# Drains in the loop, paired gathers and a reordered tail in a hard-max attention kernel

## The chip, the cores and the metric

The kernel runs on one core of a Trainium2 chip. The metric is device time in microseconds, the median of several executions. Each kernel was also run once under the hardware profiler. Runs are compared only with runs of the kernel before on the same chip, in the same rounds. Some of the experiments fell on chips that ran everything at a mean granted TensorE clock of 0.90 to 0.94 in place of about 0.95, where the kernel before takes 504 to 513 us; I call them slow chips. A drain (DRAIN in the traces) is an instruction of GpSimd's sequencer that ends only some time after the gathers issued before it.

## The reference

For each of 4 batches there are 4096 queries and 4096 keys of 128 numbers. Each query takes the value row of the key with the largest dot product.

```python
logits = np.matmul(q, k.transpose(0, 2, 1))
best = np.argmax(logits, axis=-1)
return v[b_idx, best, :].astype(np.float32)
```

## The kernel before

The queries are worked off in 128 tiles of 128 rows, one tile `t` per loop iteration `it`. TensorE and ScalarE make a score for each group of four keys, VectorE folds two halves (`fold`, tile `W`) and takes the top eight (`top`, MAX8 into `TOP`). Then three kinds of indirect DMA follow, all issued by GpSimd:

- `kg`: the group's key differences, two tiles to a group, one DMA for each tile. VectorE multiplies them with the queries (`dots`, tile `prod`) and picks the key.
- `vr`: the chosen value rows, one DMA per tile ("values").
- at the very end, rows flagged as too close are done over exactly: `FR` (their records), `FQ` (their queries), `FK` (three DMAs, candidate keys), `FV` (the exact value) and a scatter into the output. Between `FV` and the scatter stands a branch to a general path that runs only if something could not be handled (with this data it never runs).

A Python scheduler fixes the order on each engine at build time. Queues `near_q` (group gathers and their completion marks), `late_q` (values) and `fast` (flagged rows) are emptied by `issue`, once per iteration:

```python
def issue(it):
    n = 0
    clock[0] = it
    put_out(it)
    while near_q and (n < 1 + (it >= T - 28 and len(near_q) > 2) or near_q[0] in marks):
        g = near_q.pop(0)
        n += g not in marks
        g()
    if fast and it >= rest[0]:
        fast.pop(0)()
        rest[0] = it + 3
    take_late(2 if n == 0 and len(late_q) > 4 or it >= T - 24 and it % 2 == 0 else 1)
```

The condition is looked at anew for each gather: when one pair with its mark is queued (three entries), the first is issued, two entries are left, and the second has to wait for the next iteration. The mark that follows the second gather lets the group's products go into VectorE's order a fixed number of iterations later:

```python
def dots(c, x, m):
    ...
    yield "until", lambda: ("kg", x) in done, 1 if x >= TAIL else 2
    kg = kg_t.pop(x)
    prod = rp.tile([P, m, 3, P], FP16, tag=f"prod{m}", name=f"prod_{x}")
    nc.vector.tensor_tensor(out=prod, in0=kg, in1=natq[b % 2][...], op=OP.mult)
    ...
```

The end, cut:

```python
        late(LATE)                       # LATE = 8 values
        get(FR, rec, rr, P * T)
        get(FQ, q_flat, row, P * T)
        late(1)
        ...
        for r in range(3):
            get(FK[:, r, :], k_flat, gb[:, r:r + 1], B * Sk)
        ...
        late(3)
        win = whole(exact(FK, FQ, gb, 3, "fe"))
        get(FV, v_flat, win, B * Sk)
        late(1 << 20)
        ...
        all_rows()                       # reads HARD, branches
        nc.gpsimd.indirect_dma_start(out=out_flat, out_offset=IOA(ap=rowk, axis=0), in_=FV, ...)
```

## Time and profile before

| | before |
|---|---|
| time, median of the first runs | 466.72 us (466.47 to 467.32) |
| span of the profiled run | 465.5 us |
| last MAX8 starts (end of the loop) | 420.1 us |
| gather FR starts | 435.2 us |
| scatter starts | 454.4 us |
| GpSimd's last long DRAIN ends | 464.7 us |

The end of the loop, in VectorE's timeline (start and duration, in us):

```profile
420.06 1.23 DVE L232 MAX8 TOP<-W 128x8 f32<-128x1024 f32 x1
```

The page of the kernel before: busy time and share of the span of each engine, then the busy tenths in 40 slices of 11.6 us.

```profile
span 465.5 us, 6396 instructions
...
PE 380.2 (82%) x1834; PEld 168.3 (36%) x1834; DVE 417.8 (90%) x825; ACT 376.8 (81%) x437; POOL 318.1 (68%) x345
...
DVE  2689999999999999999999999999998999998330
...
POOL 8233557877677888776678876677777777767730
```

VectorE (DVE) is full from the third slice to the end of the loop. GpSimd (POOL) shows 7 or 8 tenths, and looks free. It is not: each gather costs it another 0.3 us that is not counted as busy. The timeline of GpSimd, in columns start, duration, engine, line, operation, tiles and, in brackets, the idle time before it and what ended it:

```profile
303.90 0.99 POOL L304 DMA_INDIRECT vr<-in_v_dram,win  x1 [0.30 <-issue]
305.68 0.95 POOL L250 DMA_INDIRECT kg<-k,cand  x1 [0.79 <-issue]
306.94 0.99 POOL L304 DMA_INDIRECT vr<-in_v_dram,win  x1 [0.30 <-issue]
```

One gather every 1.3 us. The same view for the tail:

```profile
441.73 1.00 POOL L498 DMA_INDIRECT FK<-in_k_dram,gb_e  x1 [0.30 <-issue]
443.03 1.04 POOL L304 DMA_INDIRECT vr<-in_v_dram,win  x1 [0.30 <-issue]
444.37 1.00 POOL L304 DMA_INDIRECT vr<-in_v_dram,win  x1 [0.30 <-issue]
447.55 1.00 POOL L498 DMA_INDIRECT FV<-in_v_dram,xw_fe  x1 [2.19 <-DVE hi L573]
454.42 1.03 POOL L534 DMA_INDIRECT out_dram<-FV,rowk_e  x1 [5.87 <-issue]
```

The last gather of values ends at 445.4, FV starts when VectorE has the index (tile `xw_fe`, ready at 447.29; the view names an instruction just behind it), and the scatter starts 5.87 us after FV's end. The span ends 10 us after the scatter was issued, though no engine is busy. What lies in these holes are instructions of GpSimd's sequencer. The view of one source line lists them, with minimum, median and maximum in ns and the first and last start. First the line of the branch, then the end of the program:

```profile
L576 POOLq INC_SWDGE_SEM  x1: 2410/2410/2410, 450.8 to 450.8; - x1
```

```profile
L806 POOLq DRAIN  x3: 46/109/10489, 454.2 to 465.2; - x3
```

A semaphore instruction takes 2.41 us, from 450.8. Of the three drains at the end, the longest takes 10.49 us: it starts at 454.19, runs while the scatter is issued (until 455.45) and ends at 464.68, 9.23 us after. I measure drains in this way throughout: from the end of the last gather or load that GpSimd issued before them to their own end.

VectorE's waits for group gathers, in columns engine, line, what for, us in total, times, longest:

```profile
DVE prod L265 <- DMA kg<-k,cand: 3.9, 3, 1.8
```

### The profile page before, as it was taken

Reading aid. Unit: us, or ns where it says so; the run is one execution under the profiler, and the core shown is the slowest. Engines: PE = TensorE matmul, PEld = TensorE weight load, DVE = VectorE, ACT = ScalarE, POOL = GpSimd, SP = SyncE. Lnnn points to the kernel's source line nnn. Section 1 sums busy time; section 2 is a strip of 40 time slices with the busy share of each in tenths; the row PEclk is TensorE's granted clock in tenths of the full one; section 3 lists DMA queues with packets and bytes.
Section 4 is the critical chain, followed back from the end, with each engine's and each line's share of the span. In section 5 each row is a group of like instructions: output and inputs, shape, how many; then the busy total and the mean of one; then the engine's idle time right before and its main releaser. Section 6 shows DMA issues by size and latency. Waiting matters only on the chain.

```text
span 465.5 us, 6396 instructions
## 1 busy us (share of the span) xinstructions
PE 380.2 (82%) x1834; PEld 168.3 (36%) x1834; DVE 417.8 (90%) x825; ACT 376.8 (81%) x437; POOL 318.1 (68%) x345
## 2 busy tenths in 40 slices
PE   8999999998999889999998889998998888850100
PEld 4444444443444344444443334443333333320000
DVE  2689999999999999999999999999998999998330
ACT  2999999999999989999997889999998888840000
POOL 8233557877677888776678876677777777767730
PEclk9999999999999999999999999999999999995555
DMA  7934576853325877943235653423432333322320
GB/s 130 227 66 96 107 103 97 139 120 85 80 76 135 148 140 128 121 126 81 79 98 137 129 116 94 100 80 87 110 101 79 86 86 99 87 71 68 94 74 4
DMA packets 43624, 47.54 MB, mean 102 GB/s; under 512 B 25000, under 2 KB 33451, under 8 KB 43584
## 3 DMA queue, kind: packets, MB, share of 16 engines
q0 software_dynamic: 18752, 30.97, 33.7%
q1 hardware_dynamic: 24832, 16.13, 13.1%
q8 instruction: 14, 0.23, 0.2%
q14 instruction: 26, 0.21, 0.2%
HBM read 39.59 MB, written 12.19 MB: 111 GB/s over the span
## 4 chain that ended last, share of the span: by engine, by line
DVE 31%; issue 23%; ACT 13%; PE 13%; DMA 9%; POOL 7%; POOLq 0%; DVEq 0%; ACTq 0%
DVE W L228 14%; ACT A L202 10%; PE psn L193 5%; DVE TOP L232 5%; PE psn L212 4%; DMA kg<-k,cand 4%; ACT E L215 4%; DMA vr<-in_v_dram,win 3%; DVE prod L265 3%; PE pd L193 3%; POOL kg L250 3%; POOL vr L304 2%; DVE D L274 2%; DVE p L269 2%; DMA natk<-in_k_dram 2%
## 5 line engine op out<-in xcount | busy, mean ns | idle before, releaser
L202 ACT ACTIVATE A<-pd 128x1024 f16<-128x1024 f32 x256 | 258.6, 1041 | 23.0 <-PE pd L193 22.7
L250 POOL DMA_INDIRECT kg<-k,cand x128 | 127.4, 995 | 85.1 <-issue 26.6
L228 DVE SCALAR_TENSOR_TENSOR W<-psn,E 128x1024 int16<-128x1024 f32 x128 | 166.0, 1297 | 7.0 <-ACT E L215 5.5
L193 PE MATMUL pd<-kT,qT 128*128 128x512 f16 x512 | 151.8, 378 | 15.7 <-ACT A L202 14.8
L193 PE MATMUL psn<-kT,qT 128*128 128x512 f16 x512 | 151.8, 378 | 15.3 <-ACT A L202 7.9
L304 POOL DMA_INDIRECT vr<-in_v_dram,win x128 | 136.6, 1067 | 39.0 <-issue 37.5
L193 PEld LDWEIGHTS <-qT 128*128 128x128 f16 x1024 | 98.4, 97 | 163.9 <-issue 76.0
L232 DVE MAX8 TOP<-W 128x8 f32<-128x1024 f32 x128 | 155.8, 1217 | 0.0
L212 PE MATMUL psn<-A,identh 128*128 128x512 f16 x512 | 152.1, 378 | 0.0
L215 ACT ACTIVATE E<-psn 128x1024 int16<-128x1024 f32 x128 | 132.2, 1033 | 5.0 <-PE psn L212 5.0
L212 PEld LDWEIGHTS <-identh 128*128 128x128 f16 x512 | 49.6, 97 | 60.8
L265 DVE TENSOR_TENSOR prod<-kg,natq 128x768 f16<-128x768 f16 x64 | 34.9, 546 | 3.9 <-DMA kg<-k,cand 3.9
L269 DVE TENSOR_TENSOR p<-prod 128x384 f16<-128x384 f16 x64 | 22.3, 349 | 0.1
L274 DVE TENSOR_REDUCE D<-p 128x6 f32<-128x192 f16 x64 | 21.5, 336 | 0.1
L173 ACT ACTIVATE kT<-uk 128x256 f16<-128x256 f32 x48 | 20.1, 419 | 0.9 <-PE uk L170 0.9
L64 POOL DMA_DIRECT2D natk<-in_k_dram x27 | 16.1, 599 | 0.9 <-POOLq L795 0.8
L67 POOL DMA_DIRECT2D natq<-in_q_dram x27 | 16.3, 605 | 0.2
L169 PE MATMUL uk<-identh,natk 128*128 128x128 f16 x96 | 15.8, 218 | 0.6 <-ACT A L202 0.6
L272 DVE TENSOR_TENSOR p<-p 128x192 f16<-128x192 f16 x64 | 15.7, 245 | 0.0
L464 PE MATMUL fp_e<-n_e,tri 128*128 128x1 f32 x2 | 0.6, 361 | 16.7 <-DVE n_e L462 16.7
L170 PEld LDWEIGHTS <-natk 128*128 128x128 f16 x96 | 9.3, 97 | 7.7 <-issue 5.3
L169 PEld LDWEIGHTS <-natk 128*128 128x128 f16 x96 | 9.3, 97 | 5.6
(147 smaller groups left out, 133.5 us busy)
## 6 DMA issues: line engine op xcount, KB each, us to landing
out_dram<-vr SPq DMA_DIRECT2D x32, 256.0 KB, 2.2
natq<-in_q_dram POOLq DMA_DIRECT2D x26, 128.0 KB, 3.2
k<-kd SPq DMA_DIRECT2D x8, 384.0 KB, 4.2
natk<-in_k_dram POOLq DMA_DIRECT2D x24, 128.0 KB, 3.9
kg<-k,cand POOLq DMA_INDIRECT x128, 2.8
vr<-in_v_dram,win POOLq DMA_INDIRECT x128, 2.8
natq<-in_q_dram POOLq DMA_DIRECT2D x1, 768.0 KB
natk<-in_k_dram POOLq DMA_DIRECT2D x1, 512.0 KB, 5.2
```

What stands on the lines that cost most here:

```text
L169: nc.tensor.matmul(out=o, lhsT=natk[b % 2][:, h, 4 * m + x, :], rhs=identh, start=True, stop=False)
L193: nc.tensor.matmul(out=ps[:, n * 512:(n + 1) * 512], lhsT=qT[b % 2][:, qt * P:(qt + 1) * P], rhs=kT[b % 2][:, u * 1024 + n * 512:u * 1024 ...
L202: nc.scalar.activation(out=A, in_=ps, func=AF.Abs)
L212: nc.tensor.matmul(out=ps[:, n * 512:(n + 1) * 512], lhsT=identh, rhs=A[:, n * 512:(n + 1) * 512], start=False, stop=True)
L215: nc.scalar.activation(out=E, in_=ps, func=AF.Relu, scale=QSCALE)
L228: nc.vector.scalar_tensor_tensor(out=W_t[t % NW].bitcast(I16)[:, 1::2], in0=ps, scalar=QSCALE, in1=E, op0=OP.mult, op1=OP.max)
L232: nc.vector.max(out=TOP[:, t, :], in_=W_t[t % NW].bitcast(FP32))
L250: near_q.append(lambda j=j: nc.gpsimd.indirect_dma_start(out=kg[:, j].rearrange("p f d -> p (f d)"), out_offset=None, in_=k16[t0 // NQT], ...
L265: nc.vector.tensor_tensor(out=prod, in0=kg, in1=natq[b % 2][:, x - b * NQT:x - b * NQT + m, :].unsqueeze(2).to_broadcast([P, m, 3, P]), op ...
L269: nc.vector.tensor_tensor(out=p1, in0=prod[:, :, :, 0:64], in1=prod[:, :, :, 64:128], op=OP.add)
L274: nc.vector.tensor_reduce(out=d[:, x - c0:x - c0 + m, 1:4], in_=p2, axis=AX_X, op=OP.add)
L304: late_q.append(lambda j=j: nc.gpsimd.indirect_dma_start(out=vr[:, j, :], out_offset=None, in_=v_flat, in_offset=IOA(ap=win[:, i + j:i + j ...
```

## The change

The intent: drains in the loop, each covering an iteration in which GpSimd is given nothing else, so that the drain at the end has less to do; group gathers in pairs when the queue is behind; the branch ahead of FV, so that its cost overlaps VectorE's exact products; the last two tiles gathered singly, so that one need not wait for the other's MAX8; the flags' first steps before the last products.

```diff
+DRAINS = (28, 60, 92)
-LATE = 8
+LATE = 7
...
-        late(3)
-        win = whole(exact(FK, FQ, gb, 3, "fe"))
-        get(FV, v_flat, win, B * Sk)
         late(1 << 20)
+        hi = fp.tile([1, 1], mybir.dt.int32, tag="hi")
+        nc.vector.tensor_copy(out=hi, in_=HARD[0:1, :])
...
-        all_rows()
+        win = whole(exact(FK, FQ, gb, 3, "fe"))
+        all_rows(hi)
+        get(FV, v_flat, win, B * Sk)
         nc.gpsimd.indirect_dma_start(out=out_flat, out_offset=IOA(ap=rowk, axis=0), in_=FV, in_offset=None,
...
@@ def issue(it)
-        while near_q and (n < 1 + (it >= T - 28 and len(near_q) > 2) or near_q[0] in marks):
+        if it in DRAINS:
+            nc.gpsimd.drain()
+            owed[0] += 2
+            return
+        behind = len(near_q) > (2 if it >= T - 28 else 4)
+        while near_q and (n < 1 + behind or near_q[0] in marks):
...
-        take_late(2 if n == 0 and len(late_q) > 4 or it >= T - 24 and it % 2 == 0 else 1)
+        more = n == 0 and len(late_q) > 4 or it >= T - 24 and it % 2 == 0
+        if owed[0] and n < 2 and it % 3 == 0 and len(late_q) > 2:
+            owed[0] -= 1
+            more = True
+        take_late(2 if more else 1)
...
@@ def gathers(t)
-            if t0 <= t < t1 and ((t - t0) % 2 or t == t1 - 1):
-                x = t0 + (t - t0) // 2 * 2
-                gather(c, x, t - x + 1)
+            m = 2 if t < T - 2 else 1
+            if t0 <= t < t1 and (t - t0) % m == m - 1:
+                gather(c, t - m + 1, m)
...
     top(T - 2)
+    gathers(T - 2)
+    flush()
     fold(T - 1)
     top(T - 1)
-    gathers(T - 2)
     gathers(T - 1)
...
         while dot:
-            two, dot = dot[:2], dot[2:]
+            if last and len(dot) == 2:
+                flags_first(T // 2, T)
+            two, dot = (dot[:1], dot[1:]) if last else (dot[:2], dot[2:])
```

Cut: tile shapes that let single and paired tiles share buffers, and bookkeeping of what is done.

More of the change, by code (lines that the diff above doesn't have):

```diff
@@ L245, in gather @@
                                 op0=OP.bitwise_and, op1=OP.bitwise_xor)
-        kg = rp.tile([P, n, 3, P], FP16, tag=f"kg{n}", name=f"kg_{t0}", bufs=8)
+        kg = rp.tile([P, 2, 3, P], FP16, tag="kg", name=f"kg_{t0}", bufs=8)[:, 0:n]
         assert len(kg_t) < 8
@@ L263, in dots @@
         kg = kg_t.pop(x)
-        prod = rp.tile([P, m, 3, P], FP16, tag=f"prod{m}", name=f"prod_{x}")
+        prod = rp.tile([P, 2, 3, P], FP16, tag="prod", name=f"prod_{x}")[:, 0:m]
         nc.vector.tensor_tensor(out=prod, in0=kg, in1=natq[b % 2][:, x - b * NQT:x - b * NQT + m, :].unsqueeze(2).to_broadcast([P, m, 3, P]),
@@ L267, in dots @@
         yield "dve",
-        p1 = rp.tile([P, m, 3, 64], FP16, tag=f"p1{m}", name=f"p1_{x}")
+        p1 = rp.tile([P, 2, 3, 64], FP16, tag="p1", name=f"p1_{x}")[:, 0:m]
         nc.vector.tensor_tensor(out=p1, in0=prod[:, :, :, 0:64], in1=prod[:, :, :, 64:128], op=OP.add)
         yield "dve",
-        p2 = rp.tile([P, m, 3, 32], FP16, tag=f"p2{m}", name=f"p2_{x}")
+        p2 = rp.tile([P, 2, 3, 32], FP16, tag="p2", name=f"p2_{x}")[:, 0:m]
         nc.vector.tensor_tensor(out=p2, in0=p1[:, :, :, 0:32], in1=p1[:, :, :, 32:64], op=OP.add)
@@ L274, in dots @@
         nc.vector.tensor_reduce(out=d[:, x - c0:x - c0 + m, 1:4], in_=p2, axis=AX_X, op=OP.add)
-        done.add(("dot", x))
+        done.update(("dot", i) for i in range(x, x + m))
     def pick(c, t0, t1):
@@ L280, in pick @@
         d = D_t[c % 4][:, 0:n, :]
-        yield "until", lambda: all(("dot", x) in done for x in range(t0, t1, 2)), 0
+        yield "until", lambda: all(("dot", x) in done for x in range(t0, t1)), 0
         cand = cand_t.pop(c)
@@ L557, in exact @@
         yield "dve", 0.17
-        win = fp.tile([P, 1], U32, tag="xw", name=f"xw_{name}")
+        win = fp.tile([P, 1], U32, tag=f"xw{R}", name=f"xw_{name}")
         nc.vector.tensor_reduce(out=win, in_=lt, axis=AX_X, op=OP.min)
@@ L569, in whole, with all_rows @@
                 return s.value
-    def all_rows():
-        hi = fp.tile([1, 1], mybir.dt.int32, tag="hi")
-        nc.vector.tensor_copy(out=hi, in_=HARD[0:1, :])
+    def all_rows(hi):
         left = nc.values_load(hi[0:1, 0:1], min_val=0, max_val=1 << 24,
@@ L679, in issue @@
             rest[0] = it + 3
-        take_late(2 if n == 0 and len(late_q) > 4 or it >= T - 24 and it % 2 == 0 else 1)
+        more = n == 0 and len(late_q) > 4 or it >= T - 24 and it % 2 == 0
[3 more added lines that the diff above has]
+        take_late(2 if more else 1)
+    owed = [0]
     def gathers(t):
         for c, (t0, t1) in enumerate(chunks):
-            if t0 <= t < t1 and ((t - t0) % 2 or t == t1 - 1):
-                x = t0 + (t - t0) // 2 * 2
-                gather(c, x, t - x + 1)
+            m = 2 if t < T - 2 else 1
+            if t0 <= t < t1 and (t - t0) % m == m - 1:
+                gather(c, t - m + 1, m)
             if t == t0:
@@ L771 @@
         dot = [s for s in live if s["kind"] == "dots" and s["c"] == c]
+        last = c == len(chunks) - 1
         while dot:
-            two, dot = dot[:2], dot[2:]
+            if last and len(dot) == 2:
+                flags_first(T // 2, T)
+            two, dot = (dot[:1], dot[1:]) if last else (dot[:2], dot[2:])
             drain(two)
-        last = c == len(chunks) - 1
-        if last:
-            flags_first(T // 2, T)
         drain([p], "cnt" if last else None)
```

## The prediction

> **What bounds it now.** In the loop (to 421 us) the page has VectorE 90%, PE 82%, ScalarE 81% busy; the windows give VectorE 59.4 of the 60 us from 360 to 420. GpSimd (68%) is nearly full too: a gather takes 1.00 to 1.07 us and the timeline shows 0.30 us "issue" before each, so 1.3 us, two per 3.05-us iteration, plus 0.6-us loads. Its gaps beyond 0.3 us sum to about 15 us between 80 and 420.
>
> The last 44 us are a serial tail. By the timeline, the chain of waits and the trace's sequencer records: gathers of group 126 at 421.8 and 423.1; eight value gathers; FR 435.22; FK from 439.12; FV gather 447.55; the branch (FV landed at 450.7, then a GpSimd semaphore instruction takes 2.41 us); the last scatter 454.42 to 455.45, landed at 456.7. Then nothing works, and the end waits for a GpSimd DRAIN that ends at 464.68, 9.2 us after the scatter was issued. A drain directly after it takes 0.11 us, one at the start 0.17, so a drain by itself is cheap; I read the 9.2 us as work left by about 324 DMAs, 28 ns each (estimate). I trust this least. The Trainium skill (Perfetto Trace Analysis, DMA Instruction - SWDGE (GPSIMD)) says a GpSimd DMA's profiled end is the end of descriptor generation, not of the transfer; the trace agrees: FV ends at 448.55 and lands 2.1 us later.
>
> **What the change does.**
> 1. Three drains, one per 32 iterations; each skips an iteration's gathers (2 x 1.3 us), made up later. Each should take 2.5 to 3 us (90 to 100 DMAs x 28 ns), covered by that iteration and by slack: a group's gathers end 4 to 7 us before its products start (under 4 us near the end). Loop effect -0.5 to +1.5 us. About 105 DMAs remain for the final drain: 3.0 instead of 9.2 us. Gain 6.2 us, all at the end.
> 2. Branch ahead of FV. After: last value gather, landing, 2.4 us, FV, landing, scatter. Today GpSimd idles 2.2 us before FV while VectorE finishes the exact products; after, one value gather fewer stands behind FK and the branch overlaps the products. From FR to the scatter's start: now 19.2 us; after, adding traced durations, 17.0. Gain 2.2 us.
> 3. Last groups by single tiles, flags first. VectorE's chain shortens by roughly 1.5 us (H and F take 0.75), but FR waits for GpSimd (435.22; its index is ready at 433.7), whose queue before FR hardly shortens. Gain 0.5 us.
> 4. Paired group gathers near the end give products more slack;  About zero.
>
> **Prediction.** 466.7 - 6.2 - 2.2 - 0.5 = 457.8 us, loop neutral. Range 454.5 to 463. Chances: faster by over 2% (below 457.4) 0.43, within 2% 0.51, slower 0.06.
>
> **What would show it.** Three GpSimd drains of 2 to 3.5 us near 108, 205 and 300 us; the final drain ending 2.5 to 4 us after the scatter's issue; the scatter starting at 451 to 453; FV after the 2.4-us instruction; last MAX8 ending within 1.5 us of 421.3; VectorE's waits for group gathers under 6 us in total (3.9 now).
>
> **What would make it wrong.** A drain that costs the same however few DMAs precede it: then each loop drain stalls GpSimd 9 us, products wait, and the end gains nothing (465 to 472). GpSimd has little slack after 305 us: a long drain at iteration 92 would push FR later.

## The result, and the profile after

The changed kernel takes 476.96 us (476.91 to 477.05, 4 runs), the kernel before 466.67 us in the same rounds. The ratio is 1.0218, with a 95% interval of 1.0201 to 1.0236: slower. (A ratio is the mean time of one kernel's fast runs, those within 1.5% of its fastest, over that of the other's fast runs of the same rounds, so not quite the ratio of the medians.)

| | before | after | difference |
|---|---|---|---|
| span of the profiled run | 465.5 | 475.2 | +9.7 |
| last MAX8 starts | 420.1 | 434.6 | +14.5 |
| from there to FR's start | 15.2 | 13.2 | -2.0 |
| FR's start to the scatter's start | 19.2 | 16.8 | -2.4 |
| last gather's end to the final drain's end | 9.23 | 8.80 | -0.43 |

The last three lines make up the tail, which is 4.8 us shorter. The loop is 14.5 us longer:

```profile
434.56 1.23 DVE L233 MAX8 TOP<-W 128x8 f32<-128x1024 f32 x1
```

The page of the changed kernel:

```profile
span 475.2 us, 6402 instructions
...
PE 383.5 (81%) x1834; PEld 168.7 (35%) x1834; DVE 420.2 (88%) x830; ACT 377.9 (80%) x437; POOL 316.2 (67%) x345
...
DVE  2689999999999999898999999988996999899730
...
POOL 9244458847778878737788866547777777766740
```

VectorE's row has 8s where it had 9s. Its waits say for what:

```profile
DVE prod L266 <- DMA kg<-k,cand: 15.4, 14, 3.7
```

15.4 us against 3.9, 14 waits against 3. Busy times from 300 to 420 us, before and after; the columns are the window, its length, then busy us (and instructions) of PE, PEld, DVE, ACT and POOL, granted clock, DMA share and GB/s:

```profile
300.00:420.00 120.00, 99.97 (x426) 40.83 (x424) 117.29 (x241) 100.00 (x107) 89.54 (x88) 0.99 0.32 88
```

```profile
300.00:420.00 120.00, 101.16 (x421) 40.65 (x420) 109.00 (x228) 99.71 (x108) 84.44 (x84) 0.99 0.31 86
```

VectorE was idle for 2.7 of these 120 us and is now idle for 11.0. Now the drains, those of the loop, then those at the end, then the branch's semaphore instruction:

```profile
L674 POOLq DRAIN  x3: 9837/10585/11913, 96.7 to 302.9; - x3
```

```profile
L818 POOLq DRAIN  x3: 46/109/10072, 464.3 to 474.9; - x3
```

```profile
L576 POOLq INC_SWDGE_SEM  x1: 2290/2290/2290, 458.5 to 458.5; - x1
```

The records of the loop's drains are 9.8 to 11.9 us long, but they begin while earlier gathers are still being issued. The timeline shows how long GpSimd stands still at the first:

```profile
100.75 1.22 POOL L305 DMA_INDIRECT vr<-in_v_dram,win  x1 [0.30 <-issue]
108.05 1.06 POOL L251 DMA_INDIRECT kg<-k,cand  x1 [6.09 <-issue]
109.42 1.01 POOL L305 DMA_INDIRECT vr<-in_v_dram,win  x1 [0.30 <-issue]
```

The gather before it ends at 101.97, the drain's record (from 96.69) at 107.27: 5.30 us. For the second and third the same subtraction gives 6.59 and 6.02 us. The Trainium skill (Perfetto Trace Analysis, Sequencer-only Instruction) says that a DRAIN's profiled window is its execution, from the moment its semaphores are satisfied. In this trace the window begins at 96.69, while earlier gathers are still being issued, so half of its length, 5.3 of 10.6 us, is a wait for the engine's earlier work.

The tail of the changed kernel, GpSimd's timeline:

```profile
454.24 1.00 POOL L499 DMA_INDIRECT FK<-in_k_dram,gb_e  x1 [0.30 <-issue]
455.54 1.06 POOL L305 DMA_INDIRECT vr<-in_v_dram,win  x1 [0.31 <-issue]
461.65 1.00 POOL L499 DMA_INDIRECT FV<-in_v_dram,xw_fe  x1 [5.05 <-DMA FK<-in_k_dram,gb_e]
464.54 1.03 POOL L536 DMA_INDIRECT out_dram<-FV,rowk_e  x1 [1.89 <-DMA FV<-in_v_dram,xw_fe]
```

FV now follows the branch, and the scatter follows FV by 1.9 us of idle time in place of 5.87. That part works as planned. The final drain hardly moved, although only 107 DMAs precede it since the last drain, where it was 324.

The four pairs of numbers in this one trace already say more. Counting GpSimd's DMAs between drains:

| | DMAs since the last drain | us after the last gather | ns per DMA |
|---|---|---|---|
| after, iteration 28 | 64 | 5.30 | 82.8 |
| after, iteration 60 | 80 | 6.59 | 82.4 |
| after, iteration 92 | 73 | 6.02 | 82.5 |
| after, end | 107 | 8.80 | 82.2 |
| before, end | 324 | 9.23 | 28.5 |

A drain is proportional to the number of DMAs, at three times the price I had assumed, and the kernel before pays for only 112 of its 324.

### The profile page after: what moved, and what is told of

Read it like the earlier page. It is cut to its first block, busy times and chain, and to the rows that moved or that the text cites. A ratio compares the mean times of both kernels' runs of the same rounds, so it can differ in the third digit from the quotient of the medians.

```text
span 475.2 us, 6402 instructions
## 1 busy us (share of the span) xinstructions
PE 383.5 (81%) x1834; PEld 168.7 (35%) x1834; DVE 420.2 (88%) x830; ACT 377.9 (80%) x437; POOL 316.2 (67%) x345
## 5 line engine op out<-in xcount | busy, mean ns | idle before, releaser
L251 POOL DMA_INDIRECT kg<-k,cand x128 | 128.3, 1002 | 98.5 <-issue 45.5
L305 POOL DMA_INDIRECT vr<-in_v_dram,win x128 | 134.1, 1048 | 39.0 <-issue 36.0
L266 DVE TENSOR_TENSOR prod<-kg,natq 128x768 f16<-128x768 f16 (+1 forms) x65 | 35.6, 548 | 15.7 <-DMA kg<-k,cand 15.4
L270 DVE TENSOR_TENSOR p<-prod 128x384 f16<-128x384 f16 (+1 forms) x65 | 22.6, 348 | 0.1
L275 DVE TENSOR_REDUCE D<-p 128x6 f32<-128x192 f16 (+1 forms) x65 | 21.9, 336 | 0.1
L273 DVE TENSOR_TENSOR p<-p 128x192 f16<-128x192 f16 (+1 forms) x65 | 16.2, 248 | 0.1
L245 DVE TENSOR_SCALAR cand<-TOP 128x2 uint32<-128x2 uint32 (+1 forms) x65 | 11.8, 182 | 0.5
L171 PEld LDWEIGHTS <-natk 128*128 128x128 f16 x96 | 9.3, 97 | 7.5 <-issue 4.8
```

The lines of the kernel that those rows point to most:

```text
L251: near_q.append(lambda j=j: nc.gpsimd.indirect_dma_start(out=kg[:, j].rearrange("p f d -> p (f d)"), out_offset=None, in_=k16[t0 // NQT], ...
L266: nc.vector.tensor_tensor(out=prod, in0=kg, in1=natq[b % 2][:, x - b * NQT:x - b * NQT + m, :].unsqueeze(2).to_broadcast([P, m, 3, P]), op ...
L270: nc.vector.tensor_tensor(out=p1, in0=prod[:, :, :, 0:64], in1=prod[:, :, :, 64:128], op=OP.add)
L275: nc.vector.tensor_reduce(out=d[:, x - c0:x - c0 + m, 1:4], in_=p2, axis=AX_X, op=OP.add)
L305: late_q.append(lambda j=j: nc.gpsimd.indirect_dma_start(out=vr[:, j, :], out_offset=None, in_=v_flat, in_offset=IOA(ap=win[:, i + j:i + j ...
```

## The experiments

Two questions: what a drain costs and when (e1 to e6, e9, e15, e16), and what lengthens the loop (e7, e8, e11 to e14, e17, e18).

### First round, on a slow chip

e1_no_drains takes the drains out of the changed kernel:

```diff
-DRAINS = (28, 60, 92)
+DRAINS = ()
```

> The changed kernel with the three loop drains taken out, all else kept. Theory A (a drain costs 82.4 ns for each GpSimd DMA since the last drain, at most about 112 of them, so the loop drains cost 18 us of GpSimd and save 0.4 us at the end): the loop is back at before's (last MAX8 starts at 420 +- 2 us, now 434.6), the final drain still ends 9.2 us after the scatter's issue, the tail gain of the other parts stays (last MAX8 to end 41 us), so 461 to 463 us. Theory B (the loss comes from the paired gathers and the new order of GpSimd's queue, the drains merely sit in slack): still 472 to 477 us.

e2_drains_only puts the drains, the skipped iterations and the values made up later into the kernel before:

```diff
+DRAINS = (28, 60, 92)
...
+        if it in DRAINS:
+            nc.gpsimd.drain()
+            owed[0] += 2
+            return
...
```

> Before with only the three drains, the skipped iterations and the values made up later. Theory A: three drains of 5.3 to 6.6 us of GpSimd standstill, loop later by 8 to 15 us, final drain shorter by only 0.4 us: 475 to 481 us. Theory B (pairing and order are at fault): 465 to 468 us.

e4_tail_only is e1 with before's rule for group gathers (the edit is shown against e1):

```diff
-        behind = len(near_q) > (2 if it >= T - 28 else 4)
-        while near_q and (n < 1 + behind or near_q[0] in marks):
+        while near_q and (n < 1 + (it >= T - 28 and len(near_q) > 2) or near_q[0] in marks):
```

> The changed kernel without the drains and with before's rule for how many group gathers an iteration issues, so only the tail's changes (single tiles at the end, branch ahead of the last value gather, fewer values held back). If the pairing is neutral, as predicted, the same as e1_no_drains within 1 us, 461 to 463 us; if the pairing costs loop time, 2 to 4 us faster than e1_no_drains; if it helps, slower than it.

All three ran on a chip where the kernel before took 503.9 to 513.2 us, at a granted clock of 0.90 to 0.93. The ratios there were 0.988 (0.978 to 0.997), 1.058 (1.049 to 1.067) and 0.994 (0.987 to 1.001). The times expected were for the other clock, so these runs decide nothing about the loop, and I ran e1 and e2 again later. The drains they hold do count: e1 and e4 end with 9.23 us after 324 DMAs, as before does, and e2 with 9.21 us after 112. (e8, which is e2 on a chip at 0.95, has the same 9.21, and 5.30, 6.44 and 5.78 us in the loop, as e2 has.)

e3_spacing moves the drains:

```diff
-DRAINS = (28, 60, 92)
+DRAINS = (72, 73, 75, 79, 87, 103)
```

> The changed kernel with drains at iterations 72, 73, 75, 79, 87 and 103 in place of 28, 60 and 92: spacings of 1, 2, 4, 8 and 16 iterations, to read a drain's cost against the number of DMAs since the last one. Theory A: from the end of the last descriptor generation the first (about 190 DMAs before it) takes 9.2 us, the cap; the others 82 ns times their DMAs, so 0.1 to 0.3, 0.4, 0.8, 1.5 and 3.2 us, and the final drain about 6 us for some 75 DMAs. Theory C (a drain also waits for the data of the last DMA to land): none of them under about 2 us. Theory D (a fixed 5 to 9 us when anything at all was issued): all six 5 us or more. The time itself is of no interest, 470 to 480 us.

| drain | DMAs since the last | us after the last DMA | 82.4 ns x DMAs |
|---|---|---|---|
| iteration 72 | 168 | 5.14 | 13.8 |
| 73 | 0 | 0.05 (its record) | 0 |
| 75 | 5 | 2.87 | 0.4 |
| 79 | 12 | 2.93 | 1.0 |
| 87 | 19 | 2.54 | 1.6 |
| 103 | 41 | 3.40 | 3.4 |
| end | 79 | 6.51 | 6.5 |

The table is worked out from single records of the trace; the view of the source line lists the six drains of the loop together:

```profile
L674 POOLq DRAIN  x6: 47/7764/8930, 241.8 to 373.2; - x6
```

The time was 517.4 us, on the slow chip. Theory D falls (41 DMAs cost less than 79, none cost nothing). Theory A's price holds for 41 and 79 DMAs. For 5, 12 and 19 there is a floor of some 2.5 to 2.9 us, as theory C has it, but that the floor is the landing of the last DMA is not shown: e3's trace records no landings, and in the page of the changed kernel gathers land 2.6 to 3.1 us after their issue starts, so 1.6 to 2.1 us after it ends. (Behind 5 and 12 DMAs the last one was a plain load.) The first line is not as expected: 168 DMAs cost 5.14 us, no more than 62 would, and not the 9.2 us of a cap.

### The count that falls

So 168 count as 62 and 324 count as 112. The differences are 106 and 212. A count that rises by one for each DMA and falls by 106 whenever it has come to some limit above 112 fits every drain measured. If that is right, a few DMAs more could make the final drain shorter. e5_pad20 and e6_pad40 add 20 and 40 dummy loads to e1, of 16 bytes for each of 128 partitions, in iterations in which GpSimd waits anyway:

```diff
+    PAD = {0: 5, 1: 5, 2: 5, 3: 5}
+    pad = cp.tile([P, 20, 4], FP32, name="pad", tag="pad")
+    def fill(it):
+        for i in range(PAD.get(it, 0)):
+            nc.gpsimd.dma_start(out=pad[:, padded[0]], in_=q[0][0:P, 0:4])
+            padded[0] += 1
...
             load_part(1, it)
+            fill(it)
```

> e1_no_drains with 20 dummy 2-KB GpSimd loads in the idle GpSimd time of the first four iterations. Six drains so far cost 82.4 ns for each DMA since the last drain (64, 70, 73, 79, 80, 107, 112 DMAs), but 168 DMAs cost only 62 times that and 324 only 112 times. Theory A1 (a count that loses 106 whenever it reaches some limit between 113 and 168): 344 DMAs give either 26 (a final drain of 2.2 to 3 us after the scatter's issue, so 6 to 7 us faster than e1) if the limit is 132 or less, or 132 (10.9 us) if it is higher. Theory A2 (a plain cap: never more than 112): 9.2 us as before, time within 0.5 us of e1.

> The same with 40 dummies, 364 DMAs in all. A1: 46 (3.8 us) if the limit is 152 or less, otherwise 152 (12.5 us). A2: 9.2 us.

Both came out as A1 had it, on a chip where before took 466.84 us. e5's final drain ends 2.36 us after the scatter's issue (26 x 82.4 ns is 2.14), e6's 3.84 us (46 x 82.4 ns is 3.79). e5 takes 459.51 us, ratio 0.983 (0.981 to 0.986); e6 461.01 us in one run. e7, the same kernel without dummies on the same chip, takes 468.60, so 20 dummies save 9.1 us, more than the 6 to 7 expected. The lines of the drain and of the semaphore instruction in e5:

```profile
L828 POOLq DRAIN  x3: 46/109/3618, 454.2 to 458.4; - x3
```

```profile
L576 POOLq INC_SWDGE_SEM  x1: 680/680/680, 449.6 to 449.6; - x1
```

The semaphore instruction has shrunk with the count too, from 2.39 us in e7 to 0.68. That is 1.7 of the 9.1 us. Over all runs it is about 0.2 us plus 20 ns times the count at that moment (one or two below the final one, for the DMAs still to come).

Where is the limit? In three traces a gap slightly longer than its neighbours stands ahead of DMA 113, 219 or 325, counted from 0. The 0.79 us shown for the kernel before is the one ahead of DMA 219; in e5, the gap ahead of DMA 325 is about 0.6 us longer than without dummies. They are 106 apart. This is a hint only: e9 and e15, below, have no longer gap ahead of DMA 113 or 325 (0.30 us, as elsewhere). On that reading the kernel before ends with the count at 112, one below the highest it can have. e9_before_pad4 tests it with the smallest change I could think of: the kernel before plus 4 dummies.

```diff
+    PAD = {0: 2, 1: 2}
```

> Before with nothing changed but 4 dummy 2-KB GpSimd loads in idle time of the first two iterations, 328 GpSimd DMAs instead of 324. In three traces a gap 0.1 to 0.5 us longer than its neighbours stands before DMA number 113, 219 and 325 (counted from 0), and the drain's account fits a count that loses 106 there: before ends on 112, the highest it can be. Theory A1: 4 more DMAs carry it over the edge to 10: final drain 2.2 to 2.8 us after the scatter's issue instead of 9.2, the semaphore instruction about 0.4 instead of 2.4 us, 457.5 to 459.5 us. Theory A2 (cap, or e5's gain came from something else): 466 to 468 us.

458.05 us against 467.37, ratio 0.981 (0.978 to 0.984), with nothing of the loop or the tail touched:

```profile
L816 POOLq DRAIN  x3: 46/109/2949, 451.5 to 455.2; - x3
```

```profile
L576 POOLq INC_SWDGE_SEM  x1: 380/380/380, 449.4 to 449.4; - x1
```

The longest drain has gone from 10.49 to 2.95 us (1.69 us after the scatter's issue, under the 2.2 to 2.8 expected), the semaphore instruction from 2.41 to 0.38. Four loads of 2 KB that nobody reads save 9 us. e16_before_pad1 adds one dummy in place of four (`PAD = {0: 1}`):

> Before with one dummy, 325 DMAs. If the count drops when DMA number 325 (from 0) is issued, one dummy does not reach it: final drain 9.3 us, 466 to 468 us. If 4 dummies helped for another reason than the count: 457 to 460 us already with one.

On a slow chip again (508.13 us, before 508.51): the final drain takes 9.31 us, which is 113 x 82.4 ns:

```profile
L816 POOLq DRAIN  x3: 46/109/10571, 494.9 to 506.0; - x3
```

One DMA does not reach the edge, four do. All the drains, with the count as n up to 113, n - 106 up to 219, n - 212 up to 325 and n - 318 from there:

| kernel | DMAs since the last drain | count | us measured | 82.4 ns x count |
|---|---|---|---|---|
| e9 | 328 | 10 | 1.69 | 0.8 |
| e5 | 344 | 26 | 2.36 | 2.1 |
| e10 (below) | 350 | 32 | 2.70 | 2.6 |
| e6 | 364 | 46 | 3.84 | 3.8 |
| e3, iteration 72 | 168 | 62 | 5.14 | 5.1 |
| before | 324 | 112 | 9.23 | 9.2 |
| e16 | 325 | 113 | 9.31 | 9.3 |

What the count is, I did not measure. The Trainium skill (DMA: Bandwidth & Descriptors, SWDGE vs HWDGE vs iDMA) says that GpSimd writes descriptors into rings; a guess is that entries of such a ring, given back in a batch when it fills and by a drain, would behave so. No run here shows a ring, and that gathers of 96 KB and dummies of 2 KB count alike is all I can add.

### What lengthens the loop

e7 and e8 repeat e1 and e2 on a chip at 0.95.

> e1_no_drains once more: its chip ran everything at a granted clock of 0.91, before at 506 us. On a chip at 0.95 I expect what e1 was to show: 461 to 463 us, last MAX8 starting at 420 +- 2 us, 9.2 us of final drain.

> e2_drains_only once more for the same reason: at a clock of 0.95, before plus 8 to 15 us, 475 to 481 us; loop drains of 5.3, 6.4 and 5.8 us after the last descriptor, final 9.2 us.

Both expectations were missed. e7 takes 468.60 us where before takes 466.84 (ratio 1.004, 1.001 to 1.007), and e8 468.93 (1.004, 1.001 to 1.007). So the drains alone cost 2 us, not 10, and all the rest without the drains costs nearly 2 us where I had expected a gain of 5. Last MAX8: 424.4 us in e7, 422.4 in e8, against 420.1. Each part is harmless; together they cost 10. Theory A was right about the drain's price and wrong about its effect: 5.3 to 6.4 us of standstill disappear almost wholly. There is slack between a gather and its products, and VectorE's order gives way too: counting in the traces how many folds (tile `W`) stand ahead of each product, e8's products come one fold later than before's after the first drain, two after the second and up to three after the third. The suspect was the new rule for group gathers, which meets the backlog after each drain. e11_unpaired is the changed kernel, drains and tail kept, with before's rule; e12_paired_before is before with the new rule alone:

```diff
-        while near_q and (n < 1 + (it >= T - 28 and len(near_q) > 2) or near_q[0] in marks):
+        behind = len(near_q) > (2 if it >= T - 28 else 4)
+        while near_q and (n < 1 + behind or near_q[0] in marks):
```

> The changed kernel with its three drains but before's rule for group gathers. Drains alone cost 2.1 us (e8), everything but the drains 1.7 us (e7), together 10.3 us. If the rule that issues two gathers when the queue is behind is what turns the drains' standstill into waits of VectorE (15.4 us of waits for group gathers against 6.1 and 6.0): 467 to 470 us and under 8 us of such waits. If drains and tail clash without it: 475 us or more.

> Before with only the new rule for group gathers (behind, fixed at the start of an iteration). If it is what costs e7 its loop time: last MAX8 at 422 to 425 us, 468 to 471 us, final drain 9.2 us. If neutral, as predicted: 466 to 467.5 us.

e11: 468.19 us against 467.37 (ratio 1.002, 0.9995 to 1.004). e12: 473.67 us (1.013, 1.010 to 1.016). The one line of the rule costs 6 us by itself, more than the 1 to 4 expected, and taking it out of the changed kernel takes back 9 of the 10 us (ratios of 1.022 and 1.002, each to before in its own rounds). VectorE's waits for group gathers in e11 and in e12:

```profile
DVE prod L266 <- DMA kg<-k,cand: 4.7, 5, 1.9
```

```profile
DVE prod L265 <- DMA kg<-k,cand: 9.4, 5, 2.6
```

From iteration 100 on, a pair and its mark make three entries, more than 2, so the new rule issues both gathers and the mark in one iteration. The products then move one iteration earlier in VectorE's fixed order. GpSimd, one gather per 1.3 us, is late by then, and VectorE waits. After a drain the same happens earlier (a limit of 4): the queue catches up in the program, while GpSimd stands still for 5 to 6 us more than the program knows. The same count of folds shows both: in e12 the products of tiles 96 to 122 stand one fold earlier than before's, all others where before's stand; in the changed kernel only one group after each drain comes a fold later and the next are back in before's place (from tile 96 on one fold ahead of it), where those of e11 stay later for longer, as in e8. To tell this from a rival (the values pushed behind the pairs are what is late), e13 and e14 keep the pairing and put the products back by one iteration, e13 in e12 and e14 in the changed kernel:

```diff
-        yield "until", lambda: ("kg", x) in done, 1 if x >= TAIL else 2
+        yield "until", lambda: ("kg", x) in done, (1 if x >= TAIL else 2) + (96 <= x < 118)    # e14: 16 <= x
```

> e12 (before with the new rule for group gathers) with the products of groups 96 to 117 one iteration later in VectorE's order. If products scheduled too early for their data are the loss: VectorE's waits for group gathers back under 5 us (9.4 in e12), last MAX8 at 419 to 422 us, 466 to 469 us. If the values behind the pairs are the loss: 472 us or more, as e12.

> The changed kernel, drains and pairing and tail kept, with the products of groups 16 to 117 one iteration later. If early products are the loss: waits for group gathers under 7 us (15.4), 467 to 471 us. If not: 475 to 478 us.

Both fell on a slow chip (before 508.51 us; ratios 1.010 and 1.028, give or take 0.8 and 0.7%), where the loop is bound otherwise: VectorE waits 14.3 us for TensorE's tile `psn` in e16 (this chip) and 31.1 in e2 (the slow chip of the first round), against 1.5 in before at 0.95. One thing on these chips I left open: two runs with drains lose more than at 0.95, e2 5.8% and e14 2.8%, at a granted clock (0.90 to 0.92) that is mostly below before's in the same rounds (0.91 to 0.93). What is said here of the loop holds for chips at 0.95. Repeated:

> As e13, for a chip at a clock of 0.95: 466 to 469 us, VectorE's waits for group gathers under 5 us and last MAX8 at 419 to 422 us if products scheduled too early are the loss; 472 us or more if the values pushed behind the pairs are.

> As e14, for a chip at a clock of 0.95: waits for group gathers under 7 us, 467 to 471 us if early products are the loss; 475 to 478 us if not.

e17: 469.35 us against 467.47 (1.004, 1.002 to 1.006), last MAX8 at 420.1, where e12 had 425.9. The time is 0.4 us over the range expected. e18: 469.24 us (1.004, 1.002 to 1.006), last MAX8 at 425.9, where the changed kernel had 434.6. The waits in e17 and in e18:

```profile
DVE prod L265 <- DMA kg<-k,cand: 3.9, 2, 2.2
```

```profile
DVE prod L266 <- DMA kg<-k,cand: 6.6, 6, 2.4
```

With drains, pairing and tail all in place, one iteration of patience takes the ratio from 1.022 to 1.004. In e17 the products of tiles 96 to 116, all but one group, stand in before's place again, and its two remaining waits are at tiles 118 and 126, which the edit leaves out. The rival falls. Two remainders stay open: e17's tail is 1.2 us longer than before's (46.7 us from the last MAX8 to the end, against 45.5), and e18's loop is still 5.9 us longer.

### A version that beats both

e10_tail_pad26 has the changed tail, no drains, before's rule for gathers and 26 dummies, chosen so that the count falls before the tail. e15_tail_pad4 has 4 dummies.

> The candidate to beat both: the changed kernel's tail (branch ahead, single tiles), no drains, before's rule for group gathers, 26 dummies, so that number 325 falls before the tail and 32 remain: final drain 2.6 us, semaphore instruction 0.8 us. If the pairing costs e1's loop its 4 us: last MAX8 at 420 to 422 us, 454 to 457 us. If the changed tail order costs them: last MAX8 at 424, 458 to 460 us.

> e10 with 4 dummies in place of 26. The final drain falls from 2.7 to 1.7 to 2.4 us, the semaphore instruction from 0.8 to 0.4 us, but the dropping of the count falls into the last DMAs: 455 to 458 us.

e10: 456.98 us against 467.37, ratio 0.978 (0.975 to 0.980), faster than both kernels by over 2%; last MAX8 at 420.4, where e5, which has dummies but the new rule, has 424.5: the 4 us that e7's loop lost were the rule's too. e15 ran on a slow chip: 495.52 us against 508.51, ratio 0.976 (0.969 to 0.983), final drain 1.70 us. The two can't be told apart. Most of the gain is the count: e9, without any change of the tail, has 0.981.

## Why the prediction was wrong

**The price of a drain: wrong, and the first step to fail.** The prediction read "the 9.2 us as work left by about 324 DMAs, 28 ns each". It had one number and divided it. The form, work per DMA, was right, and a drain with nothing before it is free, as it said. But it is 82.4 ns per DMA, and the count behind it falls by 106 on the way. So "3.0 instead of 9.2 us. Gain 6.2 us" became 8.80 and 0.43, and the loop's drains took 5.3 to 6.6 us in place of 2.5 to 3.

**"Loop effect -0.5 to +1.5 us" for the drains: nearly right.** Alone they cost 2.1 us (e8), although they are twice as long as predicted. The slack of a group's products and their later places in VectorE's order took up the rest; I did not separate the two.

**"Paired group gathers near the end give products more slack ... About zero": wrong, and the larger error.** The rule costs 6 us alone (e12) and 9 with the drains (changed kernel against e11, by their ratios to before). I looked at GpSimd's order, where a pair does come earlier, and not at what its mark does to VectorE's order: the products come earlier by a whole iteration, the data do not. The prediction named the sign to look for, VectorE's waits under 6 us; they were 15.4.

**The branch ahead of FV: the right size, but it leaned on the pairing.** FR to the scatter was predicted to go from 19.2 to 17.0 us and went to 16.8. That sum has one value behind FK in place of two. In e11, which has this tail without the pairing, three stand there, and FR to the scatter stays at 19.1 us. So the number was partly luck.

**Single tiles and flags first: the size was off.** From the last MAX8 to FR the tail is 2.0 us shorter, where 0.5 was predicted; how much of that is only GpSimd having caught up while the loop was late, I did not separate. With before's rule (e10 and e11) it is 14.0 us, 1.2 shorter than before's.

**The sum.** Predicted: loop 0, tail -8.9. Measured in the traces: loop +14.5, tail -4.8. Of the 19.2 us between 457.8 and 476.96, about 9 are the pairing on top of the drains (changed kernel against e11), about 6 the final drain that did not shrink, about 2 the drains in the loop; the rest I can't assign.

The range of 454.5 to 463 rested on both failed steps. Its stated alternative, a drain that costs the same whatever precedes it (465 to 472), was not what happened either: the final drain, 8.80 us, came near it, but the loop's drains lay between it and my reading and did little harm by themselves.

## What to carry to other kernels

A long drain at the end of a kernel is work that can be measured: place drains at several distances and fit, before building on one number divided by another. Here the account behind it falls in steps, and a kernel may end just below a step; four DMAs more then moved its end by 9 us. And when a scheduler fixes one engine's order from marks that another engine's order sets, issuing something earlier in the program moves its consumers too: look at the consumer's waits, not at the producer's queue.

## What the Trainium skill lacked or had wrong

- VectorE: DVE Perf Modes, The DRAIN you can't avoid, says that boilerplate DRAINs, before and after a kernel, are constant at about 12 ns on all five engines. The drains at the end of the kernel before are near that on VectorE, SyncE and TensorE (7 to 17 ns); ScalarE has one of 80 ns, and GpSimd's longest took 10.49 us, 9.23 us of it after its last DMA was issued, 2% of the span. The traces put these drains on the kernel's own line 806, so whether the page means them is not shown.
- No page I found gives what a drain on GpSimd costs: 82.4 ns for each GpSimd DMA in the count (5.30 us for 64, 8.80 us for 107), not under 1.7 to 2.9 us when any DMA preceded it, 0.05 us when none did.
- No page I found has the count's fall: 168 DMAs cost 5.14 us, 324 cost 9.23, 325 cost 9.31, 328 cost 1.69.
- No page I found has the semaphore instruction of GpSimd on the way past a branch: 0.38 us with 9 DMAs in the count, 2.41 us with 111.
- Perfetto Trace Analysis, Sequencer-only Instruction: it gives a DRAIN's window as its execution. On GpSimd the record starts while earlier gathers are being issued, and 5.3 of the 10.6 us of the first loop drain were that.
- DMA: Bandwidth & Descriptors, Anatomy of one DMA, puts the fixed cost of a GpSimd DMA at about 2.0 us, the writing of descriptors included. In the trace of before the gather FV landed 2.1 us after its issue ended, but 3.1 us after it began, as the issue itself took 1.0.
